# A two-layer trunk on one Trainium2 core: the opening's loads, blocks and TensorE order rewritten

## The chip, the cores and the metric

The kernel runs on one core of one Trainium2 chip. The metric is device microseconds of one execution; lower is better. Each number quoted from the trace is of one profiled execution.

## What is computed

The reference is a trunk of two layers. Each layer modulates its input by columns worked out from a condition vector, runs a mixer (gated DeltaNet in layer 0, retention in layer 1), normalizes, modulates again, runs a convolutional feed-forward net, and normalizes. Sequence length and width are 1024. Cut to what the change touches:

```python
e = jax.nn.silu(c @ cond_w + cond_b)
mod = (e @ ada_w[0] + ada_b[0])[:, None, :]
sh1, sc1, g1, sh2, sc2, g2 = jnp.split(mod, 6, axis=-1)
h = x * (1.0 + sc1) + sh1
proj = h @ gdn_w_in            # q, k, v, z and the gate inputs a, b
```

All arithmetic is float32. Matrix products are made from operands that are split into a high and a low part, three matmuls for each product (high by high, high by low, low by high).

## The kernel before

The kernel is written for a scheduler that takes the program's instructions, with their data dependencies, and decides the order on each engine; program order counts as priority. From line 728 on (`run`), the order of TensorE (PE) is written out by hand: `pq` ties each PE instruction behind the one before it, without a semaphore. In the opening, lines 152 to 690, it isn't, and the scheduler orders PE as well.

The opening runs in these steps.

1. `e` is worked out from `cond_w` (lines 177 to 205).
2. The columns `sh1` and `sc1` of layer 0 come in four groups of 256 features (`mod_loads`, `mod_mul`, `mod_sum`, lines 544 to 577). For each group, SP loads 2 MB, VectorE (DVE) multiplies and adds eight blocks (L557, L559), PE sums over the partitions (L170), and DVE adds the bias (L573, L574). Group g gives the columns of feature blocks 2g and 2g+1.
3. The input x is held as two halves of 512 rows, and each half as eight feature blocks of 128. Block (half, f) is turned by four PE transposes (`turn`, L584) into one of two PSUM buffers. For some blocks ScalarE (ACT) copies the result to SBUF at once (`hold`, L595), so that the transposes need not wait for the columns.
4. `first_h` (L598 to 604) makes the modulated block: ACT scales and shifts (L601), ACT rounds to the high part (L89), DVE subtracts for the low part (L90).
5. `first_mm` multiplies it by up to four weight blocks n: 0 is the small gate block (two matmuls, L613 with the high part and L614 with the low part), 1 to 3 are blocks of q, k and v (three matmuls each, L110 to L112). Half 0 takes all four (11 matmuls per f), half 1 takes blocks 0 and 1 (5 matmuls per f); their PSUM accumulators stay open over all eight f. The weights are loaded by `load_first` and split by `split_first` (L531).

The program's order before: group 0, blocks (0,0) and (0,1); group 1, then (0,2) and (0,3); group 2, then (0,4) and (0,5); group 3, then (1,0) to (1,3), (0,6), (0,7), and (1,4) to (1,7). Blocks (0,2) to (0,7) and (1,0) to (1,3) go through `hold`. Blocks (1,4) to (1,7) do not: `first_h` turns them itself. All loads are issued by SP in one queue. The last rows, `load_x(1, 1)`, use buffers that the rows of `load_x(1, 0)` leave free.

Behind the opening, `first_out` takes the accumulators through the convolution (DVE, L490), and `run` starts with the gates' transposes (L788) and goes on with projections (L716).

Of the kernel before, what the change touches and what calls it, by code (L numbers as in the profile page):

```python
# [12 lines left out]
ALU = mybir.AluOpType  # L13
AX = mybir.AxisListType

P = 128
D = 1024
S = 1024
KT = D // P
# [14 lines left out]
def trunk_kernel(ctx: ExitStack, tc, A):  # L34
    nc = tc.nc
    pe, act, dve, pool, sp = nc.tensor, nc.scalar, nc.vector, nc.gpsimd, nc.sync
# [9 lines left out]
    def tl(tag, shape, dt=F32, name=None):  # L46
        return sb.tile(shape, dt, tag=tag, name=name or tag, bufs=BUFS[tag])
# [7 lines left out]
    def ct(name, shape, dt=F32):  # L55
        return cp.tile(shape, dt, tag=name, name=name)
# [30 lines left out]

    def split(dst_h, dst_l, src, eng=dve):
        anchor["sp"] = act.activation(dst_h, src, AF.Copy)  # L89
        eng.tensor_tensor(dst_l, src, dst_h, ALU.subtract)  # L90
# [17 lines left out]
    def mm3(acc, w, k, hl, first, last, mm=pe.matmul):  # L108
        wh, wl = w
        mm(acc, wl[:, k], hl[0], start=first, stop=False)  # L110
        mm(acc, wh[:, k], hl[1], start=False, stop=False)  # L111
        mm(acc, wh[:, k], hl[0], start=False, stop=last)  # L112
# [47 lines left out]
    ones = ct("ones", [P, P])  # L160
# [3 lines left out]
    phalf = ct("phalf", [P, NCH])  # L164
    pool.memset(phalf, 0.5)

    def col_sum(a, n, tile):
        pt = tile()
        for j in range(n):
            pe.matmul(pt[:, j:j + 1], a[:, j * P:(j + 1) * P], ones[:, 0:1], start=True, stop=True)  # L170
        return pt

    def by_cols(banks, w, v, k):
        for j, bank in enumerate(banks):
            pe.matmul(bank[:, 0:1], w[:, j * P:(j + 1) * P], v[:, k:k + 1], start=(k == 0), stop=(k == KT - 1))

    NV = 5
    a0 = tl("wr", [P, NV * P], name="mva")
# [15 lines left out]
    ident, m_incl, m_low = [cst[:, i * P:(i + 1) * P] for i in range(3)]  # L194
# [5 lines left out]
    pt = col_sum(a0, NV, mm_tile)  # L200
# [10 lines left out]
    def bias_cols(i, j):  # L211
        return ada_b[:, i * 48 + j * 8:i * 48 + j * 8 + 8]
# [303 lines left out]
    sh1 = ct("v00", [P, KT])  # L516
    hT = [[], []]
    first = [None, GH, GH + 1, 0]
    ws = []
    accs = [None, None]  # L520
    mw = {}

    raw1 = []
    AB = 4 * GH

    def load_first(n):
        ti = first[n]
        raw1.append(tl("hTa", [P, KT * AB if ti is None else D], name="wr"))
        sp.dma_start(raw1[n], A["gdn_wab"] if ti is None else A["gdn_wqkv"][ti])

    def split_first(n):  # L531
        if first[n] is None:
            w = tl("wh", [P, KT * AB], F32R, name="wab")
            act.activation(w, raw1[n], AF.Copy)
            wv, rv = [t.rearrange("p (k n) -> p k n", n=AB) for t in (w, raw1[n])]
            dve.tensor_tensor(wv[:, :, AB // 2:], rv[:, :, AB // 2:], wv[:, :, AB // 2:], ALU.subtract)
            ws.append(wv)
# [4 lines left out]
        ws.append((kn(w[0]), kn(w[1])))  # L542

    def mod_loads(g):
        w = mw[g] = [tl("hTb" if g < 2 else "qkv", [P, HALF] if g > 1 else [P, 2, HALF], name="mvw") for _ in range(4 if g < 2 else 8)]
        for j, t in enumerate(w):
            sp.dma_start(t, A["ada0"][g][:, 2 * j:2 * j + 2] if g < 2 else A["ada0"][g][:, j])

    def mod_mul(g):
        w = mw[g]  # L550
        n = 3 * P if g == 0 else HALF
        a = tl("t2", [P, HALF], name="mva")[:, 0:n]
        bank = sc_tile() if g == 0 else None
        for k in range(KT):
            wk = w[k // 2][:, k % 2] if g < 2 else w[k]
            if k == 0:
                dve.tensor_scalar(a, wk[:, 0:n], e[:, 0:1], None, ALU.mult)  # L557
            else:
                dve.scalar_tensor_tensor(a, wk[:, 0:n], e[:, k:k + 1], a, ALU.mult, ALU.add)  # L559
            if g == 0:  # L560
                by_cols([bank], wk[:, n:], e, k)
        return a, bank

    def mod_sum(g, a, bank):
        c0 = 2 * g
        c = slice(c0, c0 + 2)
        if g == 0:
            pt = col_sum(a, 3, sc_tile)
            dve.tensor_add(sh1[:, 1:2], bank[:, 0:1], bias_cols(0, 0)[:, 1:2])
            dve.tensor_add(sh1[:, 0:1], pt[:, 2:3], bias_cols(0, 0)[:, 0:1])  # L570
        else:
            pt = col_sum(a, 4, mm_tile)
            dve.tensor_add(sh1[:, c], pt[:, 2:4], bias_cols(0, 0)[:, c])  # L573
        dve.scalar_tensor_tensor(sc1[:, c], pt[:, 0:2], 1.0, bias_cols(0, 1)[:, c], ALU.add, ALU.add)  # L574

    def mod_cols(g):
        mod_sum(g, *mod_mul(g))
# [3 lines left out]
    def turn(half, f):  # L581
        pt = mm_tile()
        for t in range(4):
            pe.transpose(pt[:, t * P:(t + 1) * P], xt[half][t][f // 4][:, f % 4 * P:(f % 4 + 1) * P], ident)  # L584
        return pt

    def hold(half, fs):
        for f in fs:
            if half == 0 and f > 3:
                if f % 2 == 0:  # L590
                    xT["w"] = tl("wr", [P, 2, HALF], name="xT")
                t = xT["w"][:, f % 2]
            else:
                t = tl("auh" if half else "xT", [P, HALF], name="xT")
            act.activation(t, turn(half, f), AF.Copy)  # L595
            xT[half, f] = t
# [9 lines left out]
    def first_mm(half, f, n):  # L606
        if accs[half] is None:
            accs[half] = [sc_tile(), sc_tile()] if half else acc4()
        acc, ht, last = accs[half][n], hT[half][f], f == KT - 1
        if n:  # L610
            mm3(acc, ws[n], f, ht, f == 0, last)
        else:
            pe.matmul(acc[0:AB], ws[0][:, f], ht[0], start=(f == 0), stop=False)  # L613
            pe.matmul(acc[0:AB], ws[0][:, f], ht[1], start=False, stop=last)  # L614

    def first_k(half, f):
        first_h(half, f)
        for n in range(2 if half else 4):
            first_mm(half, f, n)

    xt = [[tl("lane", [P, 2, HALF], name="xt") for _ in range(4)], [[None, None] for _ in range(4)]]
    xt[0] = [(t[:, 0], t[:, 1]) for t in xt[0]]

    def load_x(half, c):
        for t in range(4):
            if half:
                xt[1][t][c] = tl("auh", [P, HALF], name="xt")
            r0 = half * HALF + t * P
            sp.dma_start(xt[half][t][c], xin[r0:r0 + P, hs(c)])

    mod_loads(0)
    load_x(0, 0)
    for n in range(4):
        load_first(n)
    mod_loads(1)
    load_x(0, 1)
    m0 = mod_mul(0)
    split_first(0)
# [36 lines left out]
    prevs = {}  # L675
# [22 lines left out]
    U, DT, R, St = {}, {}, {}, {}  # L698
    cj, ir = {}, {}
    RTX = {}  # L700
    clk = [0.0]
    pin = [None]
    events = {}

    def pq(inst, cost):
        if pin[0] is not None:
            tc.add_manual_dep(inst.ins, pin[0].name,
                              mybir.DependencyInfo(mybir.DependencyClass.NoSync, mybir.DependencyReason.DATA),
                              reason="issue order")
        pin[0] = inst.ins  # L710
        clk[0] += cost

    COST = {32: 0.067, 64: 0.119, 128: 0.224, HALF: 0.229}

# [1079 lines left out]
    for nh in range(2):  # L1794
        pt = mm_tile()
# [383 lines left out]
```

## Time and profile before

| | |
|---|---|
| median of 3 runs | 2879.37 us |
| lowest, highest | 2879.37, 2886.99 us |
| span of the profiled execution, first to last instruction | 2868.4 us |
| median less span | 11.0 us |
| mean granted TensorE clock | 0.995 |

The page gives the span of the profiled execution and no time of its own; the median of the runs stands 11.0 us above the span. In rows of time order the first number is the start in us from the span's start, the second the duration of the merged run of instructions, and a bracket at the end says how long the engine sat idle before it and what ended that. PEld is the loading of a matmul's stationary operand, which lies beside other matmuls. Matmuls follow one another faster than one takes, since they are pipelined.

### The profile page before, as it was taken

How to read it: one execution, taken by the hardware profiler on the slowest of the kernel's cores; microseconds unless marked ns; L12 is line 12 of the kernel's file. 1: busy time of each engine (PE TensorE's matmuls, PEld its weight loads, DVE VectorE, ACT ScalarE, POOL GpSimd, SP SyncE). 2: the span in 40 equal slices, each digit the busy share in tenths (PEclk: the TensorE clock that was granted, in tenths of full speed). 3: DMA queues.
4: the chain of work that ended last, by engine and by line, in shares of the span. 5: the costliest groups of instructions: out<-in, count | busy, mean ns of one | idle time of the engine just before them, and what ended most of it. 6: DMA issues, size and time to landing. Idle time of an engine off the chain costs nothing.

```text
span 2868.4 us, 38930 instructions
## 1 busy us (share of the span) xinstructions
PE 2780.8 (97%) x13594; PEld 2273.7 (79%) x13594; DVE 2177.9 (76%) x3874; ACT 1298.0 (45%) x2387; POOL 499.8 (17%) x513
## 2 busy tenths in 40 slices
PE   8999999999999999999999999999999999999997
PEld 6788878887787878887788887777777788888886
DVE  6787778676788888868687656666689887777779
ACT  4664465344645444545433342222344644445543
POOL 0311321000023322000000002333201033332201
PEclk9999999999999999999999999999999999999999
DMA  7223242174255554855343364665754253444753
GB/s 279 89 96 122 92 139 90 64 255 148 96 186 176 189 181 164 299 161 182 129 147 125 118 202 153 200 209 159 256 200 150 74 195 132 144 140 165 285 184 116
DMA packets 252884, 465.30 MB, mean 162 GB/s; under 512 B 24144, under 2 KB 77776, under 8 KB 252688
## 3 DMA queue, kind: packets, MB, share of 16 engines
q1 hardware_dynamic: 218560, 408.02, 43.0%
q10 hardware_dynamic: 31488, 46.15, 4.4%
q0 software_dynamic: 2640, 8.65, 0.8%
q8 instruction: 107, 1.75, 0.2%
q14 instruction: 89, 0.73, 0.1%
HBM read 346.86 MB, written 115.87 MB: 161 GB/s over the span
## 4 chain that ended last, share of the span: by engine, by line
PE 61%; DVE 20%; DMA 9%; ACT 5%; issue 4%; POOL 1%; SPq 0%; ACTq 0%; DVEq 0%; POOLq 0%
PE acc L716 11%; PE acc L1296 6%; PE acc L110 5%; PE acc L111 4%; PE acc L112 4%; PE sc L716 4%; PE sc L1296 3%; PE acc L1596 3%; PE mm L716 2%; DVE o L1742 2%; DVE wb L90 2%; PE sc L110 2%; PE sc L112 2%; PE sc L111 2%; DMA mvw<-in_ada_w 1%
## 5 line engine op out<-in xcount | busy, mean ns | idle before, releaser
L716 PE MATMUL acc<-hT,wh 128*128 128x512 f32 x960 | 299.4, 393 | 0.0
L1596 PE MATMUL acc<-bb,ab 128*128 128x512 f32 x984 | 229.7, 392 | 7.0 <-DVE ab L90 4.7
L89 ACT ACTIVATE ab<-ar 128x512 fp32r<-128x512 f32 x210 | 131.2, 630 | 221.3 <-PE mm L303 52.1
L1596 PEld LDWEIGHTS acc<-bb,ab 128*128 128x128 f32 x984 | 183.0, 188 | 49.0 <-DVE ab L90 4.2
L716 PEld LDWEIGHTS acc<-hT,wh 128*128 128x128 f32 x960 | 182.0, 190 | 35.5
L90 DVE TENSOR_TENSOR ab<-ar,ab 128x512 fp32r<-128x512 f32 x210 | 147.4, 707 | 76.5 <-ACT ab L89 76.3
L1296 PE MATMUL acc<-T,wb 128*128 128x512 f32 x840 | 202.0, 389 | 0.4 <-DVE wb L90 0.4
L89 ACT ACTIVATE wb<-mm 128x512 fp32r<-128x512 f32 x216 | 124.4, 597 | 166.0 <-DVE mm L1350 154.5
L716 PE MATMUL acc<-hT,wl 128*128 128x512 f32 x480 | 196.2, 409 | 2.2 <-ACT sq L509 2.2
L1296 PEld LDWEIGHTS acc<-T,wb 128*128 128x128 f32 x840 | 157.5, 188 | 33.8 <-ACT o L1743 1.2
L90 DVE TENSOR_TENSOR wl<-wr,wh 128x1024 fp32r<-128x1024 f32 x98 | 122.2, 1247 | 74.6 <-ACT wh L89 74.0
L1773 POOL TENSOR_TENSOR o<-o 128x512 f32<-128x512 f32 x80 | 126.2, 1586 | 266.4 <-ACT pc L1366 173.1
L90 DVE TENSOR_TENSOR wb<-wr,wb 128x512 fp32r<-128x512 f32 x162 | 115.3, 713 | 67.6 <-ACT wb L89 67.5
L89 ACT ACTIVATE wh<-wr 128x1024 fp32r<-128x1024 f32 x98 | 103.8, 1060 | 137.1 <-PE acc L716 56.4
L1742 DVE SCALAR_TENSOR_TENSOR o<-g,vc,o 128x512 f32<-128x512 f32 (+2 forms) x176 | 148.8, 855 | 8.4 <-ACT o L1737 7.1
L90 DVE TENSOR_TENSOR wb<-mm,wb 128x512 fp32r<-128x512 f32 x216 | 144.6, 682 | 7.8 <-ACT wb L89 7.8
L89 ACT ACTIVATE wb<-wr 128x512 fp32r<-128x512 f32 x162 | 101.1, 626 | 95.4 <-PE acc L1296 27.5
L1350 DVE TENSOR_TENSOR mm<-wr 128x512 f32<-128x512 f32 x108 | 83.6, 774 | 70.3 <-DMA wr<-in_ffn_up 57.7
L716 PE MATMUL acc<-wh,hT 128*128 128x512 f32 x384 | 134.3, 412 | 2.1 <-DVE vv L90 2.1
L1366 ACT ACTIVATE pc<-acc 128x512 f32<-128x512 f32 x143 | 84.5, 591 | 108.5 <-PE acc L1296 64.1
L239 DVE SCALAR_TENSOR_TENSOR ada<-mvw,e,ada 128x512 f32<-128x512 f32 x140 | 105.4, 753 | 24.9 <-DMA mvw<-in_ada_w 24.6
L110 PE MATMUL acc<-T,wb 128*128 128x512 f32 x292 | 114.4, 392 | 3.7 <-DVE wb L90 3.6
(675 smaller groups left out, 7343.0 us busy)
## 6 DMA issues: line engine op xcount, KB each, us to landing
wr<-in_ffn_up SPq DMA_DIRECT2D x92, 512.0 KB, 3.9
mvw<-in_ada_w SPq DMA_DIRECT2D x80, 512.0 KB, 4.3
ad<-o SPq DMA_DIRECT2D x154, 256.0 KB, 2.3
ar<-ad SPq DMA_DIRECT2D x154, 256.0 KB, 3.7
Br<-in_ffn_down SPq DMA_DIRECT2D x88, 256.0 KB, 3.6
wr<-in_ret_wv SPq DMA_DIRECT2D x32, 512.0 KB, 3.6
ar<-od SPq DMA_DIRECT2D x56, 256.0 KB, 5.2
wr<-in_gdn_wqkv SPq DMA_DIRECT2D x24, 512.0 KB, 3.6
```

The source lines that it names most:

```text
L89: anchor["sp"] = act.activation(dst_h, src, AF.Copy)
L90: eng.tensor_tensor(dst_l, src, dst_h, ALU.subtract)
L110: mm(acc, wl[:, k], hl[0], start=first, stop=False)
L111: mm(acc, wh[:, k], hl[1], start=False, stop=False)
L112: mm(acc, wh[:, k], hl[0], start=False, stop=last)
L239: dve.scalar_tensor_tensor(a, wr[:, kk], e[:, k:k + 1], a, ALU.mult, ALU.add)
L716: pq(pe.matmul(out, lhsT, rhs, start=start, stop=stop), cost or COST[out.shape[-1]])
L1296: return pe.matmul(*a, skip_group_check=True, **kw)
L1366: act.activation(t, X, AF.Copy)
L1596: return pe.matmul(*args, skip_group_check=True, **kw)
L1742: dve.scalar_tensor_tensor(tv, gv[:, c0 - j:c1 - j], w[:, 2 - j:3 - j], tv, ALU.mult, ALU.add)
L1773: (dve if fp == 0 else pool).tensor_tensor(o[d], o[x], o[y], op)
```

## The change

`pq`, `pin` and `clk` move from behind the opening to its head, and all PE instructions of the opening go through them, the matmuls through a new helper `po` (in `col_sum`, `by_cols`, `first_mm` and, as `mm=po`, in `mm3`) and the transposes of `turn` directly. So PE's order in the opening is the program's. At the end `pin` is set back to none. `raw1` and `ws` become dictionaries, so that weight blocks can be loaded and split out of their order.

The program's order changes too. Weight block 1 is loaded ahead of the first rows; the first rows of half 1 are loaded ahead of modulation group 2, and the later rows of half 0 behind it. Weight block 1 is split at once, blocks 2 and 3 are split behind the high part of (0,1), and group 1 is multiplied behind its low part (`after` sets such an order on the issuing engine). Blocks of half 1 are multiplied between the groups: (1,0) and (1,1) behind the sum of group 1, (1,2) ahead of and (1,3) behind the sum of group 2, (1,4) and (1,5) around the sum of group 3.

```diff
     def split(dst_h, dst_l, src, eng=dve):
         anchor["sp"] = act.activation(dst_h, src, AF.Copy)
-        eng.tensor_tensor(dst_l, src, dst_h, ALU.subtract)
+        anchor["lo"] = eng.tensor_tensor(dst_l, src, dst_h, ALU.subtract)
...
+    clk = [0.0]
+    pin = [None]
+
+    def pq(inst, cost):
+        if pin[0] is not None:
+            tc.add_manual_dep(inst.ins, pin[0].name,
+                              mybir.DependencyInfo(mybir.DependencyClass.NoSync, mybir.DependencyReason.DATA),
+                              reason="issue order")
+        pin[0] = inst.ins
+        clk[0] += cost
+
+    def po(out, lhsT, rhs, start, stop):
+        pq(pe.matmul(out, lhsT, rhs, start=start, stop=stop), 0.0)
...
         for t in range(4):
-            pe.transpose(pt[:, t * P:(t + 1) * P], xt[half][t][f // 4][:, f % 4 * P:(f % 4 + 1) * P], ident)
+            pq(pe.transpose(pt[:, t * P:(t + 1) * P], xt[half][t][f // 4][:, f % 4 * P:(f % 4 + 1) * P], ident), 0.0)
...
     mod_loads(0)
+    load_first(1)
     load_x(0, 0)
-    for n in range(4):
-        load_first(n)
+    load_first(0)
+    load_first(2)
+    load_first(3)
     mod_loads(1)
+    load_x(1, 0)
+    mod_loads(2)
     load_x(0, 1)
+    mod_loads(3)
     m0 = mod_mul(0)
     split_first(0)
-    hold(0, range(2, 4))
+    split_first(1)
     for f in range(2):
         xT[0, f] = turn(0, f)
     mod_sum(0, *m0)
     for f in range(2):
         first_h(0, f)
-        split_first(1 + f)
-        for k in range(f + 1):
-            first_mm(0, k, 1 + f)
-        if f:
-            first_mm(0, 1, 1)
-        first_mm(0, f, 0)
-    split_first(3)
-    for f in range(2):
-        first_mm(0, f, 3)
-    mod_cols(1)
-    hold(0, range(4, 8))
-    mod_loads(2)
-    load_x(1, 0)
+        for n in range(2):
+            first_mm(0, f, n)
+    anchor["h"], anchor["h1"] = anchor["sp"], anchor["lo"]
+    for n in (2, 3):
+        with after("h"):
+            split_first(n)
+        for f in range(2):
+            first_mm(0, f, n)
+    hold(0, range(2, 4))
+    with after("h1"):
+        m1 = mod_mul(1)
+    hold(1, range(2))
+    mod_sum(1, *m1)
+    first_k(1, 0)
+    first_k(1, 1)
     first_k(0, 2)
     first_k(0, 3)
-    mod_cols(2)
-    hold(1, range(4))
-    mod_loads(3)
+    hold(1, range(2, 4))
     load_x(1, 1)
+    m2 = mod_mul(2)
+    first_k(1, 2)
+    hold(0, range(4, 8))
+    mod_sum(2, *m2)
+    first_k(1, 3)
     first_k(0, 4)
     first_k(0, 5)
-    mod_cols(3)
-    for f in range(4):
-        first_k(1, f)
-    first_k(0, 6)
-    first_k(0, 7)
-    for f in range(4, 8):
-        first_k(1, f)
+    m3 = mod_mul(3)
+    first_k(1, 4)
+    mod_sum(3, *m3)
+    first_k(1, 5)
+    for half in range(2):
+        for f in (6, 7):
+            first_k(half, f)
+    pin[0] = None
```

More of the change, by code (lines that the diff above doesn't have):

```diff
@@ L169, in col_sum @@
         for j in range(n):
-            pe.matmul(pt[:, j:j + 1], a[:, j * P:(j + 1) * P], ones[:, 0:1], start=True, stop=True)
+            po(pt[:, j:j + 1], a[:, j * P:(j + 1) * P], ones[:, 0:1], True, True)
         return pt
@@ L174, in by_cols @@
         for j, bank in enumerate(banks):
-            pe.matmul(bank[:, 0:1], w[:, j * P:(j + 1) * P], v[:, k:k + 1], start=(k == 0), stop=(k == KT - 1))
+            po(bank[:, 0:1], w[:, j * P:(j + 1) * P], v[:, k:k + 1], k == 0, k == KT - 1)
     NV = 5
@@ L518, in trunk_kernel @@
     first = [None, GH, GH + 1, 0]
-    ws = []
+    ws = {}
     accs = [None, None]
     mw = {}
-    raw1 = []
+    raw1 = {}
     AB = 4 * GH
@@ L527, in load_first @@
         ti = first[n]
-        raw1.append(tl("hTa", [P, KT * AB if ti is None else D], name="wr"))
+        raw1[n] = tl("hTa", [P, KT * AB if ti is None else D], name="wr")
         sp.dma_start(raw1[n], A["gdn_wab"] if ti is None else A["gdn_wqkv"][ti])
@@ L536, in split_first @@
             dve.tensor_tensor(wv[:, :, AB // 2:], rv[:, :, AB // 2:], wv[:, :, AB // 2:], ALU.subtract)
-            ws.append(wv)
+            ws[n] = wv
             return
@@ L541, in split_first @@
         split(w[0], w[1], raw1[n])
-        ws.append((kn(w[0]), kn(w[1])))
+        ws[n] = (kn(w[0]), kn(w[1]))
     def mod_loads(g):
@@ L610, in first_mm @@
         if n:
-            mm3(acc, ws[n], f, ht, f == 0, last)
+            mm3(acc, ws[n], f, ht, f == 0, last, po)
         else:
-            pe.matmul(acc[0:AB], ws[0][:, f], ht[0], start=(f == 0), stop=False)
-            pe.matmul(acc[0:AB], ws[0][:, f], ht[1], start=False, stop=last)
+            po(acc[0:AB], ws[0][:, f], ht[0], f == 0, False)
+            po(acc[0:AB], ws[0][:, f], ht[1], False, last)
     def first_k(half, f):
@@ L700, in trunk_kernel @@
     RTX = {}
-    clk = [0.0]
-    pin = [None]
     events = {}
[L705 to L711, printed above, removed]
     COST = {32: 0.067, 64: 0.119, 128: 0.224, HALF: 0.229}
```

## The prediction

> **What bounds the kernel now.** I read the page first, then the stretches of the opening, then the opening in order of time for each engine, and last the granted clock in single short stretches. The page says that TensorE (PE) is busy nearly all the time and carries most of the chain that ended last:
>
> ```profile
> span 2868.4 us, 38930 instructions
> ...
> PE 2780.8 (97%) x13594; PEld 2273.7 (79%) x13594; DVE 2177.9 (76%) x3874; ACT 1298.0 (45%) x2387; POOL 499.8 (17%) x513
> ...
> PE 61%; DVE 20%; DMA 9%; ACT 5%; issue 4%; POOL 1%; SPq 0%; ACTq 0%; DVEq 0%; POOLq 0%
> ```
>
> The median of the runs shown, 2879.37 us, is 11.0 us above this span. I make the sum as a difference in the opening and add it to the median. What the opening holds is seen by stretches, PE alone (start and end, length, busy us and instructions, granted clock, DMA share, GB/s):
>
> ```profile
> 32.30:40.50 8.20, 8.07 (x22) 1.00 1.04 388
> 40.50:45.00 4.50, 3.11 (x25) 1.00 1.05 386
> ...
> 50.90:54.40 3.50, 2.13 (x18) 1.00 0.17 40
> ...
> 65.30:75.30 10.00, 10.00 (x51) 1.00 0.12 48
> 75.30:78.80 3.50, 2.37 (x15) 1.00 0.00 0
> 78.80:128.00 49.20, 48.87 (x229) 1.00 0.26 86
> ```
>
> From the first large matmul to the end of the opening at 78.2 us PE idles only three times (1.4, 1.4 and 1.1 us), and behind the opening it is full. So whatever the opening's end is moved by should arrive at the end of the kernel almost whole, and there are only about 4 us of idle time to be won in it. The two idle times of 1.4 us are named on PE in order of time; the last piece is PE waiting for a low half of hT:
>
> ```profile
> 43.95 1.15 PE L584 MATMUL mm<-cst,xt 128*128 128x128 f32 x8 [1.37 <-ACT xT L595]
> ...
> 53.40 1.15 PE L584 MATMUL mm<-cst,xt 128*128 128x128 f32 x8 [1.37 <-ACT xT L595]
> ...
> 77.32 0.42 PE L614 MATMUL sc<-hT,wab 128*32 128x512 f32 x1 [0.91 <-DVE hT L90]
> ```
>
> **How I cost the change.** No matmul, transpose or copy is added or taken away: 128 matmuls of 512 columns, 64 transposes and the column sums stay. So the end of the opening is (first large matmul) + (PE work left from there) + (PE stalls), and I work out each before and after.
>
> **The start.** Before, in order of time:
>
> ```profile
> 25.68 1.44 PE L170 MATMUL sc<-ones,mva 128*128 128x1 f32 x6
> 26.98 0.67 PE L584 MATMUL mm<-cst,xt 128*128 128x128 f32 x2
> 28.12 1.97 PE L584 MATMUL mm<-cst,xt 128*128 128x128 f32 x8 [0.47 <-ACT xT L595]
> 32.36 0.80 PE L110 MATMUL acc<-hT,wl 128*128 128x512 f32 x1 [2.27 <-ACT hT L89]
> ```
>
> ```profile
> 29.39 0.78 ACT L601 ACTIVATE t<-mm,v,v 128x512 f32<-128x512 f32 x1
> ...
> 31.66 0.65 ACT L89 ACTIVATE hT<-t 128x512 fp32r<-128x512 f32 x1
> ```
>
> ```profile
> 20.30 2.89 SPq L529 DMA_DIRECT2D wr<-in_gdn_wqkv  x3
> ```
>
> ```profile
> wr<-in_gdn_wqkv SPq DMA_DIRECT2D x3, 512.0 KB, 6.9
> ```
>
> ```profile
> 20.60:32.30 11.70, 8.90 (x38) 1.00 1.03 403
> ```
>
> The DMA queues are saturated in this stretch (share 1.03, 403 GB/s): three 512 KB blocks issued (2.89-0.33)/2 = 1.28 us apart all land after 6.9 us, so each such block holds back what is behind it by 1.3 us. Block 1 now stands ahead of the four rows of half 0. Before, their last transposes ended at 26.98+0.67 = 27.65; PE needs the last row for both transposed blocks, so I put that end at about 27.95 (1.3 us later for the row, and the column sum no longer cut in between). The column sum, which ran at 25.68 before, is by the written order behind these transposes: 27.95+1.44 = 29.4. DVE needs 0.26 us for the modulation columns, ACT 0.78 (L601) and 0.65 (L89): the first matmul stands at 31.2, against 32.36: **-1.15 us**. ACT is free for it, because the two copies of blocks 2 and 3 and the splits of later weights now come behind. But those eight transposes (28.12) were done ahead of the first matmul and now are not: eight at 0.13-0.15 us are **+1.15 us** of work. The two cancel.
>
> At no cost I put: the loads of rows (1,0) and (0,1), which change places around one modulation group (the first land by about 39 us for transposes at 40, the second by 47 for transposes at 57; a late one would hold PE by 1.3 us a block); the last rows, whose issue on SP waits for the same buffers as before, some 53 us, with only the next weight load queued behind it, and which are wanted at 69; and the splits of blocks 2 and 3, now behind the halves of (0,1), since PE has ten matmuls of blocks 0 and 1 to do meanwhile (up to 1 us if that is too short). DVE's first modulation group is not far from the path:
>
> ```profile
> 33.95 1.22 DVE L90 TENSOR_TENSOR wl<-wr,wh 128x1024 fp32r<-128x1024 f32 x1
> ...
> 35.69 4.68 DVE L559 SCALAR_TENSOR_TENSOR mva<-mvw,e,mva 128x512 f32<-128x512 f32 x6
> ```
>
> Eight steps of 4.68/6 = 0.78 and two splits of 1.22 from about 33.1 us (low half of (0,1)) end at 41.8; PE with 22 matmuls and the 16 transposes that come first, and ACT with their copies, are there at 41.7. Groups 2 and 3 would be done 5 us or more ahead of their column sums.
>
> **The stalls.** Before, the scheduler puts transposes well ahead of their use, and ACT and DVE work behind other matmuls:
>
> ```profile
> 65.40 1.04 PE L584 MATMUL mm<-cst,xt 128*128 128x128 f32 x8
> ...
> 69.71 0.39 PE L613 MATMUL sc<-hT,wab 128*32 128x512 f32 x1
> ```
>
> There 3.3 us lie between the last transpose and the first use. Now PE's order is the program's, and in it blocks (1,4), (1,5), (1,6) and (1,7) read: four transposes, then at once the five matmuls that need them. Nothing behind may pass. What stands between is shown at one place of the trace:
>
> ```profile
> 74.23 0.81 ACT L601 ACTIVATE t<-mm,v,v 128x512 f32<-128x512 f32 x1
> ...
> 75.07 0.63 ACT L89 ACTIVATE hT<-t 128x512 fp32r<-128x512 f32 x1
> ```
>
> ```profile
> 75.76 0.42 PE L613 MATMUL sc<-hT,wab 128*32 128x512 f32 x1
> ```
>
> ```profile
> 76.58 0.68 DVE L90 TENSOR_TENSOR hT<-t,hT 128x512 fp32r<-128x512 f32 x1
> ```
>
> ```profile
> 46.60 0.39 PE L111 MATMUL acc<-hT,wh 128*128 128x512 f32 x1
> 46.83 0.40 PE L112 MATMUL acc<-hT,wh 128*128 128x512 f32 x1
> ```
>
> From L601's start to PE's first matmul 75.76-74.23 = 1.53 us, and about 0.08 from the transpose to ACT: 1.6 us idle. The second matmul is the one with the low half: 0.68 on DVE and two hand-overs are 0.75 after the high half, less the 0.23 that the first matmul takes (46.83-46.60): 0.5 more. So 2.1 us for each of four blocks, **8.4 us**, where the same stretch had 1.1.
>
> The other places, from these rows:
>
> ```profile
> 50.04 0.95 PE L170 MATMUL mm<-ones,mva 128*128 128x1 f32 x8
> ```
>
> ```profile
> 51.34 1.52 ACT L601 ACTIVATE t<-xT,v,v 128x512 f32<-128x512 f32 x2 [4.94 <-DVE v L574]
> 52.77 1.06 ACT L595 ACTIVATE xT<-mm 128x512 f32<-128x512 f32 x2
> ```
>
> - (1,2) follows its own transposes and those of (1,3): copy 0.53, perhaps the copy of (1,3) 0.53, L601 0.76, L89 0.6, less the 0.57 of (1,3)'s transposes: 1.5 to 2.1, and 0.5 for the low half; I take **2.3** (2.0 to 2.6).
> - (1,0), (1,1), (0,2) behind the first column sum: their copies end at about 42 us, then ACT gives a block each 0.76+0.6 = 1.4 us while PE uses one in five matmuls, 1.15: about 1.0+0.5+0.2+0.8 = **2.5** (1.4 to 3).
> - (0,4) behind the second column sum: columns 0.35, L601 0.76, L89 0.6, less the 1.15 of (1,3), and the low half: **1.8** (1.0 to 2.3).
> - (0,0)'s low half and two waits for a transposed buffer: **0.9**.
>
> Sum after: 8.4+2.3+2.5+1.8+0.9 = 15.9; before 1.4+1.4+1.1+0.1 = 4.0: **+11.9 us**. The two stalls that the edit is aimed at do go, but they were 2.7 us together, and what is late next is each block's own ACT and DVE chain.
>
> **The clock.** Stalls this dense can cost a second time (stretches of the length at which the clock changes here, PE alone):
>
> ```profile
> 41.73:45.14 3.41, 2.04 (x16) 1.00 1.04 384
> ...
> 130.50:133.91 3.41, 1.43 (x11) 1.00 0.55 220
> 133.91:137.32 3.41, 3.41 (x10) 0.50 0.48 165
> 161.20:164.61 3.41, 1.24 (x8) 1.00 0.02 5
> 164.61:168.02 3.41, 3.41 (x12) 0.50 0.00 0
> ```
>
> A stretch with 1.43 or 1.24 us of PE work is followed by 3.41 us at half clock, one with 2.04 us isn't. The new tail repeats 0.56 transposes, 1.6 idle, 0.23, 0.5 idle, 0.92: in any 3.41 us of it PE is busy 1.3 to 1.7 us, between these ends and nearer the lower. The stretch after (1,2) is like it. A half-clock stretch that falls on full matmul work costs half of 3.41, 1.7 us; on a stalled one little. I count one: **+1.7** (0 to 5).
>
> The page "TensorE: Matmul & The Clock Gate" of the Trainium skill (sections "Part 1: The HAM clock gate" and "Why this matters for your kernels") holds that the clock falls after about one whole idle window and asks only that gaps over some 3 us be avoided. By it the sum would be without the 1.7; the trace differs, since gaps of 2 us (busy 1.43 of 3.41) already cost a half-clock stretch here.
>
> Sum: -1.15+1.15+11.9+1.7 = **+13.6 us, 2893.0 us**.
>
> **The rivals.**
> - *The cover works:* half-1 blocks fill the stalls before the modulation groups as meant, and ACT runs ahead of PE everywhere, so that only the last block's chain shows (2.1). Then 2.1-4.0 = -1.9: about **2877**. For it: ACT sat idle 4.94 us ahead of 51.34, so it could do half-1 blocks there. Against: ACT can't read what PE hasn't transposed, and by the written order PE transposes (1,4) to (1,7) only at their use; it decides if that order doesn't bind the transposes, that is if the change doesn't do what it says. 0.11.
> - *Taken back later:* PE idles 2868.4-2780.8 = 87.6 us in all, some 73 behind the opening. If half of the delay ends in waits that the opening doesn't move: about **2885**. Against: 48.87 of the 49.20 us behind the opening are busy, and what PE waits for later starts from the opening's results. 0.14.
> - *The clock never falls:* the page's rule, or a window that lies well: **2891.3**. 0.20.
> - *The clock falls in four or five stretches*, on the blocks (0,6), (0,7) and behind the end: +5 instead of +1.7, and the two convolutions' DVE work ahead of the low halves (as at 77.32, 0.9): about **2898**. 0.12.
>
> **How the numbers follow.** The forecast itself has 0.43. About 0.3%, 8.6 us, is what a measurement of this kernel can tell. Slower by more (above 2888.0): nearly all of the forecast, of the last two rivals, 0.70. Within: the second rival, most of the first and the low ends of the stalls, 0.25. Faster by more would need more than the 4.0 us of stalls that there are, 0.05 for what I don't see. The range leaves out half of the first rival and the far end of the last, some 0.1 in all: from 2877 to 2902.
>
> **What would show it.** Right: PE's end of the opening at 88 to 93 us instead of 78.2; at each of (1,4) to (1,7) an L613 that waits about 1.6 us for ACT L89 and an L614 that waits 0.5 for DVE L90; the first large matmul near 31 us; the stalls of 1.37 before L584 gone; a half-clock stretch between 55 and 100 us; the rest of the page unchanged in busy times. Wrong: transposes of (1,5) ahead of the matmuls of (1,4); the end of the opening below 82 us; or an opening that is late by 12 us and a span that isn't.

## The result, and the profile after

The changed kernel takes 2898.84 us (median of 4 runs, 2896.16 to 2901.59) against 2879.37 us (4 runs, 2879.31 to 2886.99): ratio 1.0068, 95% interval 1.0055 to 1.0082. It is slower by 19.5 us, where 13.6 were forecast.

The page of the changed kernel, the lines that answer to those of before:

```profile
span 2896.6 us, 38935 instructions
...
PE 2791.8 (96%) x13594; PEld 2279.9 (79%) x13594; DVE 2181.4 (75%) x3874; ACT 1300.6 (45%) x2388; POOL 489.4 (17%) x513
...
PE 59%; DVE 20%; DMA 10%; ACT 6%; issue 5%; POOL 1%; SPq 0%; ACTq 0%; DVEq 0%; POOLq 0%
```

The engines do the same number of matmuls. The span is 28.2 us longer, more than the medians are apart. This execution took 2898.34 us, 1.7 us more than its span, and wherever a span is on record beside a time the difference is 1.7 to 1.8 us. So the profiled execution of before took some 2870.1 us, 9 us less than the median and less than any of the 78 timed executions of that kernel (the lowest took 2873.74 us). The "11.0 us above the span" that the forecast put around the program was mostly a quick execution, and differences between these two traces late in the program overstate the change. What they say of the first 100 us is read below, where both kernels do the same work.

PE in order of time, changed kernel (start, duration; in brackets the idle time ahead of the row and what ended it). The first row is the first large matmul, the last the first projection behind the opening:

```profile
32.10 1.36 PE L179 MATMUL acc<-hT,wab 128*32 128x512 f32 x2 [2.82 <-ACT hT L89]
...
74.77 0.41 PE L179 MATMUL sc<-hT,wab 128*32 128x512 f32 x1 [1.53 <-ACT hT L89]
75.50 0.42 PE L179 MATMUL sc<-hT,wab 128*32 128x512 f32 x1 [0.31 <-DVE hT L90]
...
82.33 1.36 PE L179 MATMUL sc<-hT,wab 128*32 128x512 f32 x2 [2.79 <-ACT hT L89]
...
94.00 0.41 PE L179 MATMUL sc<-hT,wab 128*32 128x512 f32 x1 [2.92 <-ACT hT L89]
95.44 0.42 PE L179 MATMUL sc<-hT,wab 128*32 128x512 f32 x1 [1.03 <-DVE hT L90]
...
99.42 1.36 PE L179 MATMUL sc<-hT,wab 128*32 128x512 f32 x2 [1.44 <-ACT hT L89]
...
102.56 0.80 PE L731 MATMUL acc<-hT,wl 128*128 128x512 f32 x1
```

In the kernel before the first projection is this row:

```profile
78.77 0.51 PE L716 MATMUL acc<-hT,wl 128*128 128x512 f32 x1
```

So the projections are **23.8 us late**. The delay then changes little: counted by the n-th matmul of the two traces it is 25.7 us at 125 us (the clock is still at half for some us behind the opening), 24.1 at 213 us, 23.9 at 522 us and 28.1 at the end. Between these two traces, then, the loss is made in the opening. Each of the blocks (1,4) to (1,7) waits ahead of its first matmul, and some again ahead of the one with the low part: 1.84, 2.79, 3.95 and 1.44, 10.0 us in all. All stalls behind the first matmul are 16.5 us (3.9 before).

The stalls are 12.6 of the 23.8 us. The rest shows in single stretches of PE (length, busy us and instructions, granted clock, DMA share, GB/s):

```profile
42.20:45.60 3.40, 1.84 (x13) 0.94 1.05 384
45.60:49.00 3.40, 3.31 (x9) 0.56 1.05 387
55.90:59.30 3.40, 0.93 (x3) 0.94 0.47 154
59.30:62.70 3.40, 3.40 (x16) 0.56 0.00 0
73.00:76.40 3.40, 1.56 (x7) 0.93 0.00 0
76.40:79.80 3.40, 3.13 (x14) 0.50 0.00 0
79.80:83.20 3.40, 0.78 (x2) 0.50 0.13 27
83.20:86.60 3.40, 3.40 (x10) 0.56 0.34 133
93.40:96.80 3.40, 1.77 (x8) 0.94 0.00 0
96.80:100.30 3.50, 1.97 (x9) 0.50 0.00 0
100.30:103.70 3.40, 3.40 (x11) 0.50 0.00 0
103.70:107.10 3.40, 3.40 (x11) 0.57 0.68 182
```

Four times in this table a thin stretch (0.93 to 1.84 us of work in 3.4) is followed by half clock. It lasts one stretch twice and three stretches twice, where PE stalls again in it: eight stretches, 27.3 us, where before shows none between its first large matmul and the projections. (In both kernels the matmuls up to about 38.3 us lie 0.43 us apart, not 0.23, though the clock reads 1.00 there; that is no difference between them.) Up to 102.56 the eight hold 3.31+3.40+3.13+0.78+3.40+1.97+2.26 = 18.25 us of work (the last lies behind); half of that, 9.1 us, is an estimate of what the lower clock costs. With the start (-0.26), the eight transposes no longer done ahead (+1.15) and the stalls (+12.6) this makes 22.6 of the 23.8 us; 1.2 us stays unexplained.

The table doesn't give a threshold. Its stretches end some 0.4 us behind the change of clock. Cut where the clock changes, the stretches ahead of the four falls hold 1.94 (with eight column sums), 0.48, 1.57 and 1.37 us of work, and two others that are as thin were not followed by half clock, the first and the third of these rows:

```profile
65.68:69.09 3.41, 1.84 (x8) 1.00 0.44 126
72.51:75.92 3.41, 1.57 (x9) 1.00 0.00 0
89.57:92.99 3.42, 1.51 (x9) 1.00 0.00 0
92.99:96.40 3.41, 1.37 (x6) 1.00 0.00 0
```

So thin stretches bring half clock often and not always; no run here shows what else decides.

### The profile page after: what moved, and what is told of

It reads as the page before. It is cut to its first block, busy times and chain, and to the rows that moved or that the text cites. A ratio compares the mean times of both kernels' runs of the same rounds, so it can differ in the third digit from the quotient of the medians.

```text
span 2896.6 us, 38935 instructions
## 1 busy us (share of the span) xinstructions
PE 2791.8 (96%) x13594; PEld 2279.9 (79%) x13594; DVE 2181.4 (75%) x3874; ACT 1300.6 (45%) x2388; POOL 489.4 (17%) x513
## 4 chain that ended last, share of the span: by engine, by line
PE 59%; DVE 20%; DMA 10%; ACT 6%; issue 5%; POOL 1%; SPq 0%; ACTq 0%; DVEq 0%; POOLq 0%
PE acc L731 10%; PE acc L1311 6%; PE acc L110 4%; PE acc L111 4%; PE acc L112 4%; PE sc L731 4%; PE sc L1311 3%; PE acc L1611 3%; PE mm L731 2%; DVE o L1757 2%; DVE wb L90 2%; DMA mvw<-in_ada_w 2%; PE sc L110 1%; PE sc L112 1%; PE sc L111 1%
## 5 line engine op out<-in xcount | busy, mean ns | idle before, releaser
L89 ACT ACTIVATE ab<-ar 128x512 fp32r<-128x512 f32 x210 | 131.1, 629 | 219.5 <-PE mm L317 49.8
L89 ACT ACTIVATE wb<-mm 128x512 fp32r<-128x512 f32 x216 | 124.4, 598 | 169.0 <-DVE mm L1365 155.7
L89 ACT ACTIVATE wh<-wr 128x1024 fp32r<-128x1024 f32 x98 | 103.6, 1059 | 134.7 <-PE acc L731 52.7
L1788 POOL TENSOR_TENSOR o<-o 128x512 f32<-128x512 f32 x80 | 113.6, 1428 | 266.7 <-ACT pc L1381 174.0
L89 ACT ACTIVATE wb<-wr 128x512 fp32r<-128x512 f32 x162 | 101.1, 626 | 94.7 <-PE acc L1311 26.3
```

What stands on the lines that cost most here:

```text
L1788: (dve if fp == 0 else pool).tensor_tensor(o[d], o[x], o[y], op)
```

## The experiments

The first theory is the prediction's: with PE's order fixed, a block's transposes stand right ahead of its matmuls, PE stalls for the chain through ACT and DVE, and the clock falls on it. Its rivals are that the new loads, or the new sequence of the blocks by itself, make the opening late. When openings without stalls still did not bring the time back, a second theory was needed (from e8 on). Each ratio is against the kernel before on the same chip, with its 95% interval.

### Free the transposes, free all, or fix the order of before

e1 takes the transposes out of the fixed order, e2 all of the opening:

```diff
-            pq(pe.transpose(pt[:, t * P:(t + 1) * P], xt[half][t][f // 4][:, f % 4 * P:(f % 4 + 1) * P], ident), 0.0)
+            pe.transpose(pt[:, t * P:(t + 1) * P], xt[half][t][f // 4][:, f % 4 * P:(f % 4 + 1) * P], ident)
...
-        pq(pe.matmul(out, lhsT, rhs, start=start, stop=stop), 0.0)
+        pe.matmul(out, lhsT, rhs, start=start, stop=stop)
```

(the second pair in e2 alone). e3 keeps the fixing but puts back the loads and the program order of before.

> The changed kernel, with the transposes of the x blocks taken out of the written TensorE order (matmuls and column sums stay in it). Start of the first projection matmul behind the opening: 78.8 us before, 102.6 us after the change. Theory (transposes that stand right ahead of their matmuls expose the ScalarE and VectorE chain, and the idle time halves the clock): the scheduler puts them ahead again, the opening ends at 82 to 87 us, time 2878 to 2885. Rival S (the program's order, half-1 blocks between the groups, is itself too slow): stays at 98 us or more, 2894 or more. Rival L (the load order and the later start are at fault): the same as S.

> The changed kernel with no written TensorE order in the opening at all; loads and program order stay as changed. Theory: opening ends at 77 to 84 us, time 2876 to 2884. Rivals S and L: 95 us or more, above 2890, since what they blame is still there.

> The kernel before with its own loads and program order, but TensorE's order in the opening fixed to that program order. Theory: the four blocks (1,4) to (1,7) are again transposed right ahead of their matmuls, and each modulation sum stands ahead of matmuls that could have run: opening ends at 95 to 104 us, time 2893 to 2901. Rivals S and L: 78 to 82 us, 2877 to 2883, since neither the new order nor the new loads are in it.

Measured: e1 2885.52 us, 1.0022 [1.0011, 1.0034], projections from 80.88 us; e2 2882.21 us, 1.0012 [1.0001, 1.0023], from 82.25; e3 2891.62 us, 1.0038 [1.0023, 1.0054], from 92.90. Freeing the transposes alone takes 21.7 of the 23.8 us out of the opening, and fixing the order of before puts 14.1 in, without any new load or sequence; under the fixed order the new sequence and loads add the other 9.7, and left free (e2) 3.5. e1 and e3 end the opening earlier than expected (82 to 87 and 95 to 104), and their times miss the ranges by 0.5 us upward and 1.4 downward; the rivals' figures for the opening (98 or more, 78 to 82) are far off. So the first theory holds for the opening, with the sequence as a smaller part. But e1 and e2 stay a little slower than before, and something comes behind the opening: in both PE waits for the gates' column g (2.98 and 2.33 us at 98 us).

### Keep the fixed order, but turn the last blocks one block ahead

```diff
     first_k(0, 4)
+    xT[1, 4] = turn(1, 4)
     first_k(0, 5)
     m3 = mod_mul(3)
+    xT[1, 5] = turn(1, 5)
     first_k(1, 4)
     mod_sum(3, *m3)
     first_k(1, 5)
-    for half in range(2):
-        for f in (6, 7):
-            first_k(half, f)
+    xT[1, 6] = turn(1, 6)
+    first_k(0, 6)
+    xT[1, 7] = turn(1, 7)
+    first_k(0, 7)
+    first_k(1, 6)
+    first_k(1, 7)
```

> The changed kernel, order still fixed by hand, but blocks (1,4) to (1,7) are each transposed a block of half 0 (or one block) earlier, into the second buffer: (1,4) ahead of the matmuls of (0,5), (1,5) ahead of those of (1,4), (1,6) ahead of (0,6), (1,7) ahead of (0,7). Theory: of the stalls of 1.8, 2.8, 4.0 and 1.4 us ahead of these blocks less than 2 us in all are left, and the half-clock stretches at 76 to 87 us and behind 97 us go: opening ends at 85 to 91 us, time 2880 to 2889. Rivals S and L: 98 us or more.

Measured: projections from 85.37 us, as expected; the blocks (1,4) to (1,7) no longer stall, and 0.97 us ahead of (0,6) is all that is left from there on. But the time was missed: 2892.40 us, 1.0049 [1.0030, 1.0068]. Behind the opening PE now waits 7.01 us for g, with 10.2 us of half clock that begins in the wait. e7 does the same for every block and has the same wait, shown below with e12.

### The clock by itself

e5 puts six matmuls, whose result nothing reads, into each of five waits:

```diff
+    def fill(n):
+        junk = mm_tile()
+        for _ in range(n):
+            po(junk, ws[1][0][:, 0], hT[0][0][0], True, True)
...
         first_h(half, f)
+        if half and f in (2, 4, 5, 6, 7):
+            fill(6)
```

> The changed kernel with six unused matmuls of 512 columns added ahead of the matmuls of (1,2) and (1,4) to (1,7), in the places where TensorE waits (30 matmuls more; their result is never read). At full clock six take 1.4 us, less than each of those waits. If the half clock comes from the idle time there (theory): the half-clock stretches at 59, 76 to 87 and 97 to 107 us go, the waits' ends stay about where the ScalarE chain puts them, the opening ends at 94 to 98 us instead of 102.6, time 2886 to 2893 although there is more work. Rival (the clock does not depend on it, or the waits alone cost the time): opening ends at 102 to 106 us, time 2898 or more.

Measured: with 30 matmuls more the projections start at 98.07 us, 4.5 us earlier than in the changed kernel. Two stretches of half clock are left of the eight:

```profile
63.90:67.30 3.40, 3.31 (x8) 0.53 0.54 154
91.20:94.60 3.40, 3.40 (x12) 0.53 0.00 0
```

One of the six that went, the first (from 45.2 us), isn't owed to these matmuls: none of them stands ahead of it, and e4, which has none at all, shows no half clock there either. Still, more work in the waits made the opening shorter, so the half clock is a cost of its own, above the stalls. The opening's end just misses its range (94 to 98), and the median missed it clearly (2886 to 2893): 2897.02 us (2889.13 to 2899.42), 1.0057 [1.0039, 1.0075], not distinguishable from 1.0068; the profiled execution was the quickest of its four.

### The loads alone, and every block turned ahead

e6 is the kernel before with the new order of loads alone; e7 is the fixed order with each block turned ahead (of its opening the edit of e4 is the tail), and it loads the first rows ahead of weight block 1 again. Cut:

```diff
+    def ahead(half, f):
+        xT[half, f] = turn(half, f)
...
     first_k(0, 2)
+    ahead(1, 2)
     first_k(0, 3)
-    hold(1, range(2, 4))
+    ahead(1, 3)
     load_x(1, 1)
```

> The kernel before with the new order of the loads alone (block 1 ahead of the first rows, rows of half 1 ahead of modulation group 2); program order and free TensorE order as before. Theory: the loads cost and win little: first large matmul at 32 to 34 us, opening ends at 77 to 81 us, time 2877 to 2884. Rival L (the load order is at fault): opening ends at 85 us or more.

> TensorE's order still fixed by hand, but written so that each block is transposed one block or more ahead of its matmuls, half-1 blocks go from the transposing buffer without a copy, the sum for group 0 stands behind the first two blocks as in the change, and the first rows are loaded ahead of weight block 1 again. Theory: first large matmul at 29 to 31 us, stalls behind it under 4 us in all, no half-clock stretch in the opening, opening ends at 71 to 76 us, time 2870 to 2879 unless the gates' chain behind the opening comes late as in the run with the tail turned ahead (a wait of 7 us there; then up to 2888). Rival S (half-1 blocks between the groups are too slow in any order): opening ends at 80 us or later.

Measured: e6 2880.12 us, 1.0003 [0.9994, 1.0013], though its projections start at 84.40, 5.6 us late, later than expected (77 to 81) and close to what the rival had (85 or more). By 155 us the delay is 1.6 us: before waits 1.98 us for DVE at 132.66 and then has 3.4 us of half clock, while e6 waits 0.33 us there, at full clock. The loads cost nothing that can be measured, and a later opening can be given back. e7: projections from 78.95 (71 to 76 were expected), with 2.9 us of stalls in all, but 2890.78 us, 1.0037 [1.0024, 1.0050], above all that was expected. An opening as quick as that of before costs 11.6 us somewhere behind it.

e6 also shows a stretch that fell to half clock though PE was busy in it:

```profile
51.50:54.90 3.40, 2.62 (x21) 0.96 0.00 0
54.90:58.30 3.40, 2.71 (x13) 0.50 0.24 51
```

The 21 instructions are 13 transposes and 8 column sums; no wide matmul is among them. The page "TensorE: Matmul & The Clock Gate" of the Trainium skill (section "Part 4: PE-mode transpose") holds that transposes don't count for the clock as matmuls do. The row fits that and doesn't show it, since it may be the column sums that didn't count; and against it, in the prediction's stretch of the kernel before from 41.73 to 45.14, 15 transposes make 2.00 of the 2.04 us of work, and no half clock followed.

### Where the time behind the opening goes: the gates' chain

The gates' chain runs from the copy of half 1's gate accumulator on ACT through small steps on both engines, with three table loads on ACT, to g. The next four kernels write that chain ahead of the convolutions: e8 (on e7; Silu ordered behind the gates' Ln as well), e9 (e8 with six unused matmuls ahead of the first large one), e10 (the kernel before, its opening's program untouched), e11 (e8, DVE's convolution steps also ordered behind the gates).

```diff
-        for n, acc in enumerate(accs[half]):
-            first_out(n, half, acc)
+        first_out(0, half, accs[half][0])
...
+    head = gates()
+    for _ in range(3):
+        next(head)
+    for half in range(2):
+        for n, acc in enumerate(accs[half][1:]):
+            first_out(1 + n, half, acc)
```

In e11, besides:

```diff
-            dve.scalar_tensor_tensor(oh, raw[:, 3 - j:515 - j], w[:, 3 - j:4 - j], oh, ALU.mult, ALU.add)
+            with after("gl"):
+                dve.scalar_tensor_tensor(oh, raw[:, 3 - j:515 - j], w[:, 3 - j:4 - j], oh, ALU.mult, ALU.add)
```

> The kernel with every block turned ahead, and with the gates' arithmetic written ahead of the convolutions and all Silu activations of the convolutions ordered behind the gates' Ln, so that ScalarE changes its tables three times without a Silu between. Theory (behind the opening TensorE's written order meets the gates' column g, and there it waited 7.0 us because ScalarE switched tables between gates and Silu; the wait then halved the clock for 10.2 us): that wait falls under 2.5 us, no half-clock stretch follows it, the opening ends at 78 to 80 us, time 2876 to 2884. Rival (the later loss has another cause): the matmuls fall behind by some 8 us between 80 and 190 us all the same, time 2888 or more.

> As the run with the gates first, with six unused matmuls of 512 columns added where TensorE waits for the first block (28 to 30.6 us; their result is never read). Theory: the clock comes up one stretch of 3.4 us earlier, about eight of the first matmuls take 0.23 instead of 0.43 us, the opening ends 1 to 2 us earlier, at 76.5 to 79 us; time 2874 to 2883, hardly to be told from the run beside it. Rival: the clock comes up at about 37 us as without them.

> The kernel before, its opening untouched and its TensorE order free, with nothing but the gates' arithmetic written ahead of the convolutions (without the order for Silu), which makes the scheduler put a Silu between the gates' activations on ScalarE: six table loads where it had three. Theory (the gates' place on ScalarE costs time by itself): the opening ends at 78 to 80 us as before, then TensorE waits 3 to 8 us for g near 91 us and half clock follows; time 2883 to 2893. Rival (only a fixed order in the opening brings that loss): no such wait, 2876 to 2883.

> This is the kernel of e8 (hand-fixed order, every block turned a block ahead, gates' first part written ahead of the convolutions) in which DVE's three convolution steps are also ordered behind the gates' last step on DVE. Theory (TensorE waits for the gates' column g because the gates' small steps queue behind convolution work, on ACT and on DVE): the copy of the half-1 gate accumulator stays near 78 to 80 us, g is done by 88 us, TensorE's wait for g falls from 9.5 us to under 2 us, no half clock near 95 us, the first 100 us end no later than in the kernel before plus 3 us, and the time falls from 2888.7 to 2877 to 2884 us. Rival (the three table loads of ACT alone make the chain long, or the gates' columns are late because the half-1 gate accumulator itself is read late): the wait stays at 5 us or more and the time at 2886 to 2892. Second rival (the delay comes from the convolutions that are now later, since the projections wait for their results): no wait for g, but other waits of 5 us or more before 130 us and a time of 2886 or more.

Measured: e8 2888.68 us, 1.0031 [1.0021, 1.0042]; e9 2890.32 us, 1.0039 [1.0026, 1.0052]; e10 2891.00 us, 1.0042 [1.0025, 1.0058]; e11 2889.78 us, 1.0043 [1.0029, 1.0057]. In e8 and e9 the wait for g became longer, 9.49 and 9.47 us: the three table loads of ACT now lie together, but the gates' small steps on DVE stand between convolution steps. So table loads as the only cause fall. The unused matmuls of e9 bring the step from 0.43 to 0.23 us between matmuls forward from about 36.4 us (e8) to 32.1, as its theory had it, and the projections by 0.7 us; in the time they bring nothing that can be measured. e10 shows the loss with the opening's program untouched (PE, and ACT's copy of half 1's gate accumulator):

```profile
104.11 1.09 PE L715 MATMUL mm<-g,cst 128*128 128x64 f32 x4 [11.01 <-DVE g L803]
```

```profile
83.67 0.59 ACT L681 ACTIVATE ab<-sc 32x512 f32<-32x512 f32 x1 [5.99 <-PE sc L614]
```

ACT sat idle 5.99 us ahead of that copy, where half 0's convolutions ran before; they now come behind the gates. Part of this is PE's own order, which is free in e10: projections stand ahead of the last block's matmuls, and its low part starts at 83.23 us, where it started at 77.32 before. In e11 g is there in time, and the wait moves to the convolutions, as its second rival had it (PE, in order of time):

```profile
90.14 0.63 PE L745 MATMUL mm<-g,cst 128*128 128x64 f32 x4 [0.81 <-DVE g L833]
```

```profile
105.56 1.11 PE L748 MATMUL acc<-cst,qkv 128*128 128x128 f32 x4 [6.70 <-ACT qkv L507]
113.74 1.11 PE L748 MATMUL acc<-cst,qkv 128*128 128x128 f32 x4 [7.07 <-ACT qkv L507]
```

In these kernels, whichever of the two goes first, the other is late. That suggests that ACT and DVE can't do both between the end of the opening and the time PE wants them, unless half 0's part is done before.

### Half 0 first

That gives the second theory a number. The lead is the time between ACT's copies of the two gate accumulators, half 0 (`acc`) and half 1 (`sc`). Before:

```profile
70.60 0.59 ACT L681 ACTIVATE ab<-acc 32x512 f32<-32x512 f32 x1 [2.07 <-PE acc L614]
...
77.77 0.59 ACT L681 ACTIVATE ab<-sc 32x512 f32<-32x512 f32 x1 [1.54 <-PE sc L614]
```

```profile
91.15 0.55 PE L716 MATMUL mm<-g,cst 128*128 128x64 f32 x4
```

A lead of 7.17 us, and no wait for g. What has to fit in it is seen in the changed kernel, DVE's nine convolution steps of half 0, 4.19+2.07 = 6.3 us:

```profile
90.60 4.19 DVE L504 SCALAR_TENSOR_TENSOR qkv<-raw,vc,qkv 128x512 f32<-128x512 f32 x6 [6.40 <-ACT qkv L502]
...
95.31 2.07 DVE L504 SCALAR_TENSOR_TENSOR qkv<-raw,vc,qkv 128x512 f32<-128x512 f32 x3
```

In e7 the lead is 4.14 us, and ACT's tables change back and forth between the gates (L825 to L829) and Silu (L505), each load 1.28 us:

```profile
73.83 0.57 ACT L719 ACTIVATE ab<-acc 32x512 f32<-32x512 f32 x1
...
77.97 0.57 ACT L719 ACTIVATE ab<-sc 32x512 f32<-32x512 f32 x1
...
87.03 1.28 ACT L825 ACT_TABLE_LOAD   x1
88.59 1.28 ACT L505 ACT_TABLE_LOAD   x1
...
91.60 1.28 ACT L828 ACT_TABLE_LOAD   x1
93.17 1.28 ACT L505 ACT_TABLE_LOAD   x1
```

```profile
98.52 1.09 PE L744 MATMUL mm<-g,cst 128*128 128x64 f32 x4 [7.02 <-DVE g L832]
```

Among the kernels that keep the program order behind the opening, the wait goes by the lead: 4.14 us in e4 and e7 (7.0 us of waiting), 5.53 and 5.74 in e2 and e1 (2.3 and 3.0), 7.18 in e6, 12.2 in the changed kernel, 13.6 in e5 and 21.0 in e3 (none). It goes so roughly, since e1 has more lead than e2 and waits longer. e12 tests it: e7 with one change, the blocks (1,4) to (1,7) put behind (0,7) as before, and (1,2) and (1,3) used to cover the second and third column sum. The second part of its edit, against e7:

```diff
+    mod_sum(3, *m3)
+    first_k(1, 3)
+    ahead(1, 4)
+    first_k(0, 6)
     ahead(1, 5)
+    first_k(0, 7)
     first_k(1, 4)
-    mod_sum(3, *m3)
-    first_k(1, 5)
     ahead(1, 6)
-    first_k(0, 6)
+    first_k(1, 5)
     ahead(1, 7)
-    first_k(0, 7)
     first_k(1, 6)
     first_k(1, 7)
```

> This is the kernel of e7 (hand-fixed order, every block turned a block ahead, its opening 0.2 us later than before's in the trace) with one thing changed in the order of blocks: half 0 is finished first, as in the kernel before, and the blocks (1,4) to (1,7) all come behind (0,7). The second column sum is then covered by (1,2), the third by (1,3). From the traces, the gate accumulator of half 0 is copied 7.17 us before that of half 1 in the kernel before, 7.18 us in the one with new loads alone (time unchanged), 5.74 and 5.53 us where the transposes or all were set free (time up by 0.2 and 0.1 per cent), 4.14 us in e4 and e7 (waits of 7.0 us for the gates' column g behind the opening). Theory: what is lost behind the opening is the lead with which half 0 is finished, since ACT and DVE do half 0's convolutions in it. Expected: lead 7 us or more, end of the opening at 79 to 82 us (up to 2 us more stalls at the third sum), wait for g under 2 us and no other wait above 3 us before 120 us, no half clock of 10 us there; time 2876 to 2884 us, the same as before. Rival (the order fixed by hand or the new load order costs it otherwise): a wait of 5 us or more for g or for a convolution's result remains and the time is 2887 to 2892 us.

Measured: 2878.38 us, 0.9994 [0.9982, 1.0007], 12.4 us below e7; lead, end of the opening, wait and time are all as expected. The lead is 9.73 us and PE doesn't wait for g:

```profile
70.80 0.57 ACT L719 ACTIVATE ab<-acc 32x512 f32<-32x512 f32 x1
...
80.53 0.59 ACT L719 ACTIVATE ab<-sc 32x512 f32<-32x512 f32 x1 [0.57 <-PE sc L179]
```

```profile
93.90 0.55 PE L744 MATMUL mm<-g,cst 128*128 128x64 f32 x4
```

The projections start at 81.53 us, 2.6 us later than in e7, and the kernel is still quicker. The second theory is borne out, and its rivals (the fixed order, the new loads) fall: e12 has the fixed order, and the new loads but for the first rows, which stand as in e7. It is one kernel, in which the order of the blocks had to change with the lead. The wait of e7 (7.0 us) and half clock on 6.0 us of work behind it (3.0 us) less those 2.6 explain 7.4 of the 12.4 us. By the n-th matmul e12 is 7.5 us ahead of e7 at 100 us of before's trace, and 2.7 at the end: both profiled executions were the slowest of their kernels. The rest isn't attributed. No version beats the kernel before by more than can be measured.

## Why the prediction came out as it did

- **Slower, inside the range:** right, 5.8 us above the forecast. The number came out nearer than its parts: the opening was late by 23.8 us, not 13.6. The cause named was the cause: under a fixed order each late block's chain through ACT and DVE stands open on PE. Freeing the transposes alone (e1) took 21.7 of 23.8 us out of the opening.
- **What moves the opening's end arrives whole:** right for the changed kernel between the two traces, as the n-th matmuls show; the medians moved by 4.3 us less than the opening. It is no rule of this program: e6's 5.6 us were given back, and e7, with no delay in the opening, lost 11.6 us behind it. The prediction looked at PE behind the opening, full for 49 us, and not at ACT and DVE, which need the lead of half 0.
- **The start:** -1.15 us forecast, -0.26 measured. The column sum ended at 29.27, as worked out (29.4). Two things were in the way. DVE began the modulation columns only at 29.76, some 0.4 us late, behind the low half of weight block 1:

```profile
28.62 1.23 DVE L90 TENSOR_TENSOR wl<-wr,wh 128x1024 fp32r<-128x1024 f32 x1 [0.65 <-ACT wh L89]
```

  And what failed is "ACT 0.78 (L601) and 0.65 (L89)": ACT made both blocks' scaled copies first,

```profile
30.08 1.45 ACT L615 ACTIVATE t<-mm,v,v 128x512 f32<-128x512 f32 x2 [1.49 <-DVE v L588]
31.42 1.14 ACT L89 ACTIVATE hT<-t 128x512 fp32r<-128x512 f32 x2
```

  so that the first high part waited for a second copy, 0.67 us.
- **The stalls:** 15.9 us forecast behind the first matmul, 16.5 measured; against before +11.9 and +12.6. That the sum fits so well is partly luck: the four last blocks took 10.0 us (8.4 forecast) and (1,2) 2.96 (2.3), and the places behind the first and second column sums 1.36 (2.5) and 1.56 (1.8). Single blocks differ: (1,4) and (1,7) took 1.84 and 1.44 (2.1 each forecast); (1,5) and (1,6) took 2.79 and 3.95, because ACT put other work ahead of their high part, the scaled copies of (0,6) and (0,7) or half 0's convolution copies:

```profile
79.57 0.78 ACT L615 ACTIVATE t<-mm,v,v 128x512 f32<-128x512 f32 x1 [4.85 <-PE mm L598]
80.25 1.51 ACT L615 ACTIVATE t<-xT,v,v 128x512 f32<-128x512 f32 x2
81.66 1.66 ACT L89 ACTIVATE hT<-t 128x512 fp32r<-128x512 f32 x3
```

  The first row also shows the cause by itself: ACT had nothing to do for 4.85 us and could not start, since PE had not yet been let at the transposes.
- **The clock, the term that was mis-sized:** "I count one: +1.7 (0 to 5)". Seven stretches at half clock lay in the opening and one behind, worth about 9 us before the projections start. That thin stretches bring it on was right; that work of 1.43 us does and of 2.04 doesn't was no threshold, since here 1.51 and 1.84 us were not followed by half clock and 1.57 and 1.94 were. What was missed is that four places fell, not one, and that two of them lasted 10.2 us, with PE stalling again at half clock. The term is 7.4 of the 10.2 us by which the opening came out later than forecast. The medians are only 5.8 us above the forecast. The other 4 us stay open; part may be the quick execution in which before was profiled, since e10, whose opening has the same program, has 6.8 us of half clock from 42.95 us on and ran the same matmuls 2.6 us later from 50 to 75 us.
- **The rivals:** "the cover works" decided on whether the order binds the transposes; it does, and the stalls of all four blocks are there. "Taken back later" didn't come in the traces, and at most 4.3 us of it in the medians. "The clock never falls" is ruled out by the eight stretches. "Four or five stretches", 2898 us, is the nearest in time, with fewer stretches than there were. The Trainium skill's page "TensorE: Matmul & The Clock Gate" (section "Why this matters for your kernels") asks only that gaps of more than some 3 us be avoided. The traces differ: no gap of the opening behind its first matmul was longer than 2.92 us, and the clock fell four times.

## What to carry to other kernels

An order fixed by hand must hold the distance that the scheduler had kept: a step that another engine has to answer (here a transpose) goes ahead of the step that needs the answer, here by one block. Look at the stalls of such an order together and not one by one: here 12.6 us of short stalls brought half clock worth about 9 us more. And a stage's end isn't its only result: ask which engine was doing the next stage's work under it, and whether the new order still leaves that engine its lead.

## What was not expected of the hardware

In the changed kernel's opening half clock came though no gap in PE's work behind the first matmul was longer than 2.92 us. Of its six stretches that began at full clock and held less than 2 us of work in 3.41, four were followed by it and two weren't. Transposes and column sums filling 2.62 of 3.40 us didn't hold the clock (e6), while transposes filling 2.00 of 3.41 us did in before. With six matmuls put into each of five waits (e5) two stretches of half clock were left of eight. The idle time of 7 to 11 us behind the opening came in e4, e7, e8, e9 and e10 with 10.2 us at half clock each time, some of it within the idle time itself.

Executions of one kernel spread by 5 us (the changed one) to 17 us (e12), and a single trace can mislead by as much: e12's profiled execution was the slowest of its ten (2889.17 us against a median of 2878.38), and that of before was 9 us quicker than its median.
